# Latent attention: the products with the values taken for two query tiles at once, and the preparation of the next pair of heads moved to other steps

## The chip, the cores and the metric

One core of one Trainium2 chip. The time is device microseconds of one execution of the whole program, the median of three runs.

## What is computed

The program runs two layers of a hybrid attention network on 512 tokens, then two mixers that also carry a context of 256 tokens. The change is in the first of these, the latent mixer (MLA). Cut to what matters:

```
q = (rms_norm_2(cq, q_norm_g) @ w_uq).reshape(b, n, 16, 64 + 32)     # per head: 64 plain columns, 32 rotated
kv = (rms_norm_2(ckv, kv_norm_g) @ w_ukv).reshape(b, n, 16, 64 + 64) # keys (64, + 32 shared rotated) and values (64)
s = jnp.einsum('bqhrd,bkhd->bhrqk', qi, k) * scale                    # all keys, no mask
p = jax.nn.softmax(s, axis=-1)
o = jnp.einsum('bhrqk,bkhe->bqhre', p, v)
```

The 256 context queries attend to the 256 context keys; the 512 token queries attend to all 768 keys. All is float32.

## The kernel before, in words

The 16 heads are taken as eight head pairs `hp`. A head pair has five steps: step c (both context query tiles of 128 at once, 256 keys) and steps t0 to t3 (one tile of 128 token queries each, 768 keys). Four generators make the work of a step:

- `softmax` writes the scores of each of the two heads into a PSUM bank pair `S` (two buffers) with `mm3`, which multiplies two-part operands in three passes (lines 282 to 284). VectorE takes the row maximum (L1220), ScalarE the exponential (L1225), VectorE the reciprocal (L1227) and the scaling (L1230); the result is the tile `p`, queries down, keys across.
- `weigh` turns the `p` of the step before: TensorE transposes it in blocks of 128x128 into banks `T` (three buffers of one bank, L1245), ScalarE copies them to `pt` (L1246), and TensorE multiplies them with the values `V` into the bank `O` (one buffer, L1253): for each block of 128 keys one matmul per head, the two heads in the two halves of the array's columns, 64 value columns stationary, 128 queries moving. One such float32 matmul leaves two records in the trace. VectorE then multiplies `O` into the gate `sg` (L1260).
- `prepare(hp + 1)` makes the keys `kT` and queries `qT` of the next head pair: four matmul groups (six when the next pair is even, with a rotation of the queries on VectorE, L1176 to L1181), whose results go from a `T` bank through `split` (a copy on ScalarE, L253 or L256, then a difference on VectorE, L254 or L257) to SBUF. Four DMAs on SP's queue bring the rotated rows from `rot` into `qT`.
- `values` fills `V` before the first step.

The loop over steps calls these generators in turn: `next(sm)`, `next(ready)`, `next(w)`, twice a step. So the preparation of the next pair goes beside steps c, t0 and, if long, t1, until it is used up. A scheduler then sets each engine's order: an instruction that is ready may be moved ahead of one that waits. Engines run their own order strictly.

Names on the profile's rows: `S<-kT,qT` are scores; `T<-ident,p` transposes; `O<-pt,V` products with the values; `T<-ckT,spl` and `T<-cqT,spl` preparation. A similar scheme with two query tiles at a time stands already in the first layers' attention (`pt` with four blocks of 2x128, written at L521 and used at L528).

Of the kernel before, what the change touches and what calls it, by code (L numbers as in the profile page):

```python
# [10 lines left out]
F32 = mybir.dt.float32  # L11
# [3 lines left out]
AF = mybir.ActivationFunctionType  # L15
# [783 lines left out]
def alternate(*parts):  # L799
    parts = list(parts)  # L800
    while parts:
        parts = [p for p in parts if next(p, parts) is not parts]
# [256 lines left out]
def mla(P, xs, mod, H, before, keep):  # L1059

    nc, A = P.nc, P.A
# [13 lines left out]
    with ExitStack() as s1:  # L1075
# [33 lines left out]
        for j in range(8):  # L1109
            w = W().rearrange("p s (k n) -> p s k n", k=8)  # L1110
            for c, o, n in PARTS:
                ps = P.bankA()[:, 0:n]
                for k in range(8):
                    P.mm3(ps, w[:, 0, k], w[:, 1, k], *H.all(k, c), k == 0, k == 7)
                v = sg[j][:, o:o + n]
# [3 lines left out]
    before.close()  # L1119
    with st as s2:  # L1120
        P.psum(s2, S=(2, 2), T=(3, 1), O=(1, 1))
        kp, pp, one, qp = (P.pool(*x, s2) for x in (("m2k", 3), ("m2p", 3), ("m2o", 1), ("m2q", 4)))
        kTs = [one.tile([96, 2, 768], F32R, name=f"kT{i}") for i in (2, 3, 0, 1)]
        kTs = kTs[2:] + kTs[:2]
        tab = one.tile([128, 512], F32, name="tab")
# [1 line left out]
        V = [vp.tile([128, 1024], F32, name="V") for _ in range(6)]  # L1127
# [7 lines left out]
        for c, o, n in PARTS:  # L1135
            pt = P.bankT()
# [71 lines left out]
        def softmax(hp, c, t0):  # L1208
            two, m, c0 = (2, 256, 512) if c else (1, 768, 0)
            ps = []  # L1210
            for i in range(2):
                qT, kT = qTs[hp][i], kTs[(2 * hp + i) % 4]
                pss = P.bankS()
                for t in range(two):
                    q = slice(c0 + (t0 + t) * 128, c0 + (t0 + t + 1) * 128)
                    for o, w in ((512, 256),) if c else ((0, 512), (512, 256)):
                        d = pss[:, t * m + o - c0:t * m + o - c0 + w]
                        P.mm3(d, qT[:, 0, q], qT[:, 1, q], kT[:, 0, o:o + w], kT[:, 1, o:o + w], True, True)
                mx = P.sm.tile([128, 2], F32, name="mx")
                nc.vector.tensor_reduce(mx[:, 0:two], pss[:, 0:two * m].rearrange("p (t n) -> p t n", t=two),  # L1220
                                        AX.X, OP.max, negate=True)
                p = pp.tile([128, 768], F32, name="p")
                sl = P.sm.tile([128, 2], F32, name="sl")
                for t in range(two):
                    nc.scalar.activation(p[:, t * m:(t + 1) * m], pss[:, t * m:(t + 1) * m], AF.Exp,  # L1225
                                         bias=mx[:, t:t + 1], accum_out=sl[:, t:t + 1])
                nc.vector.reciprocal(sl[:, 0:two], sl[:, 0:two])  # L1227
                for t in range(two):
                    v = p[:, t * m:(t + 1) * m]
                    nc.vector.tensor_scalar(v, v, sl[:, t:t + 1], None, op0=OP.mult)  # L1230
                ps.append(p)
                yield ps

        def weigh(hp, c, t0, ps):
            two, m, c0 = (2, 256, 512) if c else (1, 768, 0)
            if t0 == 0:
                weigh.o = P.bankO()
            pts = []
            for p in ps:
                pt = kp.tile([128, 768], F32, name="pt")  # L1240
                for o in range(0, two * m, 512):
                    w = min(512, two * m - o)
                    pst = P.bankT()
                    for k in range(0, w, 128):
                        nc.tensor.transpose(pst[:, k:k + 128], p[:, o + k:o + k + 128], P.ident)  # L1245
                    nc.scalar.activation(pt[:, o:o + w], pst[:, 0:w], AF.Copy)  # L1246
                pts.append(pt)
                yield
            for t in range(two):
                for k in range(m // 128):  # L1250
                    for i in range(2):
                        h = 2 * hp + i
                        nc.tensor.matmul(weigh.o[64 * i:64 * i + 64, (t0 + t) * 128:(t0 + t + 1) * 128],  # L1253
                                         V[4 * c + k][:, h * 64:(h + 1) * 64],
                                         pts[i][:, t * m + k * 128:t * m + (k + 1) * 128],
                                         start=(k == 0), stop=(k == m // 128 - 1))
            n = 256 if c else 512
            if (t0 + two) * 128 == n:
                v = sg[hp][:, c0:c0 + n]
                nc.vector.tensor_tensor(v, v, weigh.o[:, 0:n], op=OP.mult)  # L1260
# [3 lines left out]
        for hp, c, t in steps:  # L1264
            if c:
                ready = prepare(hp + 1) if hp < 7 else iter(())
            sm = softmax(hp, c, t)
            w = weigh(*before) if before else iter(())
            next(w, None)
            for _ in range(2):  # L1270
                ps = next(sm)
                next(ready, None)
                next(w, None)
            before = (hp, c, t, ps)
        alternate(weigh(*before))


# [325 lines left out]
def program(tc, A, out):  # L1603
    with ExitStack() as ctx:
        P = Prog(tc, A, ctx)
        xs = [P.res.tile([128, 1024], F32, name=f"x{t}") for t in range(4)]
        before, keep = ExitStack(), ExitStack()
        H, mod = first_block(P, xs, P.pool("hx", 1, before))
        finish = mla(P, xs, mod.m[0], H, before, keep)
        gla(P, xs, finish, keep, mod.m[1], out)  # L1610
# [18 lines left out]
```

## Time and profile before

| what | value |
|---|---|
| median of 3 runs | 2325.97 us (2324.53 to 2327.81) |
| profiled execution, own time | 2323.18 us |
| its span, first to last instruction | 2321.4 us |
| TensorE busy | 2270.4 us, 98% |
| VectorE busy | 1477.5 us, 64% |
| ScalarE busy | 1064.0 us, 46% |
| latent mixer, first score to last product with values | 1674.96 to 1926.59 us |

Shares are means over the whole program, so the table says only which engine is busiest; the rows below are of the one stretch that the change touches.

### The profile page before, as it was taken

The numbers are of one execution on the slowest core, as the hardware profiler recorded it, in microseconds if no ns is written. First come the engines' busy times: TensorE is split into PE (matmuls) and PEld (weight loads), VectorE is DVE, ScalarE is ACT, GpSimd is POOL, SyncE is SP. The second block draws the span as 40 slices with busy tenths as digits, with TensorE's granted clock in tenths as the row PEclk, the third lists the DMA queues.
The fourth block names the chain that finished last, engine by engine and source line by source line (L and its number), as shares of the span: only waits on it lengthen the run. The fifth ranks groups of instructions, "written<-read, shape, count | busy, mean of one in ns | idle before, by whom it ended". The sixth has DMA issues, their size and how long they took to land.

```text
span 2321.4 us, 30494 instructions
## 1 busy us (share of the span) xinstructions
PE 2270.4 (98%) x11980; PEld 1866.9 (80%) x11980; DVE 1477.5 (64%) x2556; ACT 1064.0 (46%) x1958; POOL 71.4 (3%) x120
## 2 busy tenths in 40 slices
PE   8999999999999999999999999999999999999998
PEld 6777878888888777787888888888888888788886
DVE  4477795455555547779645556564477776756586
ACT  3366423444443336632344445452467773563332
POOL 0000000000000000000000000010000000000000
PEclk9999999999999999999999999999999999999999
DMA  4221464545542222146455554212110121121111
GB/s 154 82 75 54 156 214 139 173 127 156 170 100 91 83 82 82 46 163 214 131 178 126 159 165 116 92 54 71 50 31 20 26 74 37 53 83 37 55 47 72
DMA packets 61311, 234.37 MB, mean 101 GB/s; under 512 B 8544, under 2 KB 9840, under 8 KB 54768
## 3 DMA queue, kind: packets, MB, share of 16 engines
q1 hardware_dynamic: 50512, 179.99, 23.3%
q0 software_dynamic: 3456, 25.17, 6.0%
q10 hardware_dynamic: 7200, 27.27, 3.7%
q8 instruction: 94, 1.54, 0.3%
q14 instruction: 49, 0.40, 0.1%
HBM read 227.15 MB, written 2.10 MB: 99 GB/s over the span
## 4 chain that ended last, share of the span: by engine, by line
PE 69%; DVE 7%; ACT 2%; issue 2%; DMA 1%; POOL 1%; POOLq 0%; ACTq 0%; DVEq 0%; SPq 0%
PE A L282 14%; PE A L284 14%; PE A L283 14%; PE S L282 4%; PE S L283 4%; PE S L284 4%; PE O L1253 2%; PE T L1245 2%; DVE spl L254 1%; DMA ada<-in_ada 1%; PE O L284 1%; PE O L282 1%; PE O L283 1%; POOL rstd L293 1%; PE T L282 1%
## 5 line engine op out<-in xcount | busy, mean ns | idle before, releaser
L282 PE MATMUL A<-big,spl 128*128 128x512 f32 (+1 forms) x1280 | 482.3, 377 | 1.9 <-DVE x L777 1.2
L284 PE MATMUL A<-big,spl 128*128 128x512 f32 (+1 forms) x1280 | 479.9, 375 | 0.2 <-DVE spl L254 0.2
L283 PE MATMUL A<-big,spl 128*128 128x512 f32 (+1 forms) x1280 | 479.3, 375 | 0.0
L254 DVE TENSOR_TENSOR spl<-raw,spl 128x1024 fp32r<-128x1024 f32 (+2 forms) x265 | 317.2, 1200 | 181.4 <-ACT spl L253 179.6
L253 ACT ACTIVATE spl<-raw 128x1024 fp32r<-128x1024 f32 (+2 forms) x265 | 274.4, 1037 | 295.3 <-PE A L284 196.8
L282 PEld LDWEIGHTS A<-big,spl 128*128 128x128 f32 x1280 | 241.1, 188 | 47.3 <-issue 3.5
L284 PEld LDWEIGHTS A<-big,spl 128*128 128x128 f32 x1280 | 241.1, 188 | 43.8 <-issue 1.6
L283 PEld LDWEIGHTS A<-big,spl 128*128 128x128 f32 x1280 | 241.3, 188 | 41.1
L254 DVE TENSOR_TENSOR spl<-quarter,spl 128x1024 fp32r<-128x1024 f32 x84 | 102.2, 1223 | 144.5 <-ACT spl L253 144.5
L282 PE MATMUL A<-spl,big 128*128 128x512 f32 (+2 forms) x480 | 182.5, 383 | 7.4 <-ACT spl L253 3.4
L283 PE MATMUL A<-spl,big 128*128 128x512 f32 (+2 forms) x480 | 181.6, 379 | 0.5 <-DVE ms L291 0.5
L284 PE MATMUL A<-spl,big 128*128 128x512 f32 (+2 forms) x480 | 181.0, 378 | 0.2 <-DVE ms L291 0.2
L253 ACT ACTIVATE spl<-quarter 128x1024 fp32r<-128x1024 f32 x84 | 88.2, 1057 | 98.0 <-PE S L284 40.2
L282 PEld LDWEIGHTS A<-spl,big 128*128 128x128 f32 x480 | 90.1, 189 | 27.0 <-ACT spl L253 5.7
L283 PEld LDWEIGHTS A<-spl,big 128*128 128x128 f32 x480 | 90.6, 189 | 17.3 <-DVE spl L254 1.8
L284 PEld LDWEIGHTS A<-spl,big 128*128 128x128 f32 x480 | 90.5, 188 | 16.5 <-DVE ms L291 0.9
L282 PE MATMUL S<-spl,part 128*128 128x512 f32 x264 | 102.7, 389 | 0.0
L283 PE MATMUL S<-spl,part 128*128 128x512 f32 x264 | 102.7, 389 | 0.0
L284 PE MATMUL S<-spl,part 128*128 128x512 f32 x264 | 102.7, 389 | 0.0
L1220 DVE TENSOR_REDUCE mx<-S 128x1 f32<-128x768 f32 (+1 forms) x80 | 71.9, 900 | 26.3 <-PE S L284 25.5
L293 POOL TENSOR_TENSOR rstd<-ms,mhalf 128x1 f32<-128x1 f32 (+2 forms) x68 | 44.2, 650 | 1239.4 <-DVE ms L291 1194.0
L1246 ACT ACTIVATE pt<-T 128x512 f32<-128x512 f32 (+1 forms) x144 | 66.5, 501 | 32.0 <-PE T L1245 31.0
(442 smaller groups left out, 4329.1 us busy)
## 6 DMA issues: line engine op xcount, KB each, us to landing
raw<-in_wl SPq DMA_DIRECT2D x196, 512.0 KB, 4.0
ada<-in_ada ACTq DMA_DIRECT2D x48, 512.0 KB, 4.3
quarter<-in_wq SPq DMA_DIRECT2D x24, 1024.0 KB, 5.5
quarter<-in_wq POOLq DMA_DIRECT2D x24, 1024.0 KB, 9.0
raw<-in_gla SPq DMA_DIRECT2D x33, 512.0 KB, 3.8
raw<-in_mla SPq DMA_DIRECT2D x20, 512.0 KB, 3.6
raw<-in_mla SPq DMA_DIRECT2D x8, 384.0 KB, 3.0
qT<-rot SPq DMA_DIRECT2D x32, 96.0 KB, 2.8
```

The lines of the kernel that those rows point to most:

```text
L253: nc.scalar.activation(hi, src, AF.Copy)
L254: nc.vector.tensor_tensor(lo, src, f32(hi), op=OP.subtract)
L282: mm(ps, lh, rh, start=start, stop=False, **more)
L283: mm(ps, lh, rl, start=False, stop=False, **more)
L284: mm(ps, ll, rh, start=False, stop=stop, **more)
L293: nc.gpsimd.tensor_tensor(r, ms, self.mhalf[:, 0:w], op=OP.pow)
L1220: nc.vector.tensor_reduce(mx[:, 0:two], pss[:, 0:two * m].rearrange("p (t n) -> p t n", t=two), AX.X, OP.max, negate=True)
L1245: nc.tensor.transpose(pst[:, k:k + 128], p[:, o + k:o + k + 128], P.ident)
L1246: nc.scalar.activation(pt[:, o:o + w], pst[:, 0:w], AF.Copy)
L1253: nc.tensor.matmul(weigh.o[64 * i:64 * i + 64, (t0 + t) * 128:(t0 + t + 1) * 128], V[4 * c + k][:, h * 64:(h + 1) * 64], pts[i][:, t * m + ...
```

## The change

`weigh` keeps one pair of `pt` tiles for two token steps (shape 128 x 6 x 2 x 128: key block, tile, query) and multiplies only in steps with odd `t0`, for both query tiles at once: 256 queries moving per matmul. Step c does the same with its two tiles. The pool of `pt` tiles grows from three of 768 to four of 1536 columns. In the loop, `ready` (the preparation) is no longer advanced in step c, in step t2, and in step t0 of even pairs; what is left of it after step t3 is drained there. `weigh` runs one step late, so the products of t0 and t1 fall in step t2, and those of t2 and t3 in the next pair's step c.

```diff
-        kp, pp, one, qp = (P.pool(*x, s2) for x in (("m2k", 3), ("m2p", 3), ("m2o", 1), ("m2q", 4)))
+        kp, pp, one, qp = (P.pool(*x, s2) for x in (("m2k", 4), ("m2p", 3), ("m2o", 1), ("m2q", 4)))
...
-            pts = []
-            for p in ps:
-                pt = kp.tile([128, 768], F32, name="pt")
+
+            if t0 % 2 == 0:
+                weigh.pts = [kp.tile([128, 6, 2, 128], F32, name="pt") for _ in range(2)]
+            pts = weigh.pts
+            for p, pt in zip(ps, pts):
...
-                    nc.scalar.activation(pt[:, o:o + w], pst[:, 0:w], AF.Copy)
-                pts.append(pt)
+                    if c:
+                        d, v = pt[:, 0:2], pst.rearrange("p (t k n) -> p k t n", t=2, k=2)
+                    else:
+                        d, v = pt[:, o // 128:(o + w) // 128, t0 % 2], pst[:, 0:w].rearrange("p (k n) -> p k n", n=128)
+                    nc.scalar.activation(d, v, AF.Copy)
                 yield
-            for t in range(two):
+            if c or t0 % 2:
+                q = slice(0, 256) if c else slice((t0 - 1) * 128, (t0 + 1) * 128)
                 for k in range(m // 128):
                     for i in range(2):
                         h = 2 * hp + i
-                        nc.tensor.matmul(weigh.o[64 * i:64 * i + 64, (t0 + t) * 128:(t0 + t + 1) * 128],
-                                         V[4 * c + k][:, h * 64:(h + 1) * 64],
-                                         pts[i][:, t * m + k * 128:t * m + (k + 1) * 128],
+                        nc.tensor.matmul(weigh.o[64 * i:64 * i + 64, q], V[4 * c + k][:, h * 64:(h + 1) * 64],
+                                         pts[i][:, k].rearrange("p t n -> p (t n)"),
...
+            busy = c or t == 2 or (t == 0 and hp % 2 == 0)
             for _ in range(2):
                 ps = next(sm)
-                next(ready, None)
+                if not busy:
+                    next(ready, None)
                 next(w, None)
+            if t == 3:
+                for _ in ready:
+                    pass
```

Counted in TensorE's order over the stretch (a block is a run of products with the values that nothing interrupts):

| | before | after |
|---|---|---|
| products with the values | 448 of 128 queries | 224 of 256 queries |
| blocks | 56 | 34 |
| blocks with an odd number of products | 32 | 20 |
| blocks entered from scores or preparation / from transposes | 53 / 3 | 29 / 5 |
| blocks left into scores or preparation / into transposes | 32 / 24 | 16 / 18 |

**Inside a head pair.** TensorE, first head pair, the change of step from t2 to t3; before:

```order
L1245 MATMUL T<-ident,p 128x128 x6
L282 MATMUL S<-kT_12798,qT 128x512
L283 MATMUL S<-kT_12798,qT 128x512
L284 MATMUL S<-kT_12798,qT 128x512
L282 MATMUL S<-kT_12798,qT 128x256
L283 MATMUL S<-kT_12798,qT 128x256
L284 MATMUL S<-kT_12798,qT 128x256
L1253 MATMUL O<-pt,V 64x128 x12
L282 MATMUL S<-kT_12795,qT 128x256
```

and now, in the same head pair, where the products of t0 and t1 stand in step t2:

```order
L1247 MATMUL T<-ident,p 128x128 x6
L282 MATMUL S<-kT_12798,qT 128x256
L283 MATMUL S<-kT_12798,qT 128x256
L284 MATMUL S<-kT_12798,qT 128x256
L1259 MATMUL O<-pt,V 64x256 x12
L1247 MATMUL T<-ident,p 128x128 x6
L282 MATMUL S<-kT_12797,qT 128x512
L283 MATMUL S<-kT_12797,qT 128x512
L284 MATMUL S<-kT_12797,qT 128x512
```

The same twelve products are twice as wide and stand once where they stood twice; three scores now lie between the last transposes and the first product instead of six.

**The first step of all.** TensorE, the scores of step c of the first head pair and what follows; before:

```order
L283 MATMUL T<-ckT,spl 128x512
L284 MATMUL T<-ckT,spl 128x512
L282 MATMUL S<-kT_12798,qT 128x256
L283 MATMUL S<-kT_12798,qT 128x256
L284 MATMUL S<-kT_12798,qT 128x256
L282 MATMUL S<-kT_12798,qT 128x256
L283 MATMUL S<-kT_12798,qT 128x256
L284 MATMUL S<-kT_12798,qT 128x256
L1245 MATMUL T<-ident,p 128x128 x4
```

and now:

```order
L284 MATMUL S<-kT_12797,qT 128x256
L282 MATMUL S<-kT_12798,qT 128x256
L283 MATMUL S<-kT_12798,qT 128x256
L284 MATMUL S<-kT_12798,qT 128x256
L282 MATMUL S<-kT_12798,qT 128x256
L283 MATMUL S<-kT_12798,qT 128x256
L284 MATMUL S<-kT_12798,qT 128x256
L1247 MATMUL T<-ident,p 128x128 x4
```

The seven matmuls of preparation between the scores of the first head and those of the second (the last two are shown) are gone from there.

**From an odd head pair to the next.** TensorE, the end of step t3 of the second head pair and step c of the third; before:

```order
L284 MATMUL S<-kT_12796,qT 128x256
L1245 MATMUL T<-ident,p 128x128 x6
L1253 MATMUL O<-pt,V 64x128
L282 MATMUL S<-kT_12797,qT 128x256
L283 MATMUL S<-kT_12797,qT 128x256
L1253 MATMUL O<-pt,V 64x128 x11
L1245 MATMUL T<-ident,p 128x128 x6
```

and now:

```order
L284 MATMUL T<-cqT,spl 128x512
L1247 MATMUL T<-ident,p 128x128 x12
L1259 MATMUL O<-pt,V 64x256
L282 MATMUL S<-kT_12797,qT 128x256
L283 MATMUL S<-kT_12797,qT 128x256
L284 MATMUL S<-kT_12797,qT 128x256
L282 MATMUL S<-kT_12797,qT 128x256
L283 MATMUL S<-kT_12797,qT 128x256
L284 MATMUL S<-kT_12797,qT 128x256
L1259 MATMUL O<-pt,V 64x256 x11
```

Preparation now ends right ahead of the transposes, and the transposes of both heads follow each other; this stands so at the end of the second, fourth and sixth head pair.

## Rows read from the trace of the kernel before

**Rows 1.** The page: the span, and TensorE's busy time, share and instructions

```profile
span 2321.4 us, 30494 instructions
PE 2270.4 (98%) x11980; PEld 1866.9 (80%) x11980; DVE 1477.5 (64%) x2556; ACT 1064.0 (46%) x1958; POOL 71.4 (3%) x120
```

**Rows 2.** Busy time of PE, PEld, DVE, ACT, POOL in the stretch; then TensorE's clock

```profile
1674.96:1926.59 251.63, 249.03 (x2088) 209.63 (x2086) 193.05 (x367) 183.53 (x417) 0.00 (x0) 1.00 0.14 35
```

**Rows 3.** Timeline of TensorE around one block: start us, us, engine line op

```profile
1818.33 0.28 PE L283 MATMUL S<-kT,qT 96*128 96x256 f32 x1
1818.45 0.28 PE L284 MATMUL S<-kT,qT 96*128 96x256 f32 x1
1818.66 1.53 PE L1253 MATMUL O<-pt,V 128*64 128x128 f32 x24
1820.12 0.50 PE L282 MATMUL S<-kT,qT 96*128 96x512 f32 x1
1820.46 0.40 PE L283 MATMUL S<-kT,qT 96*128 96x512 f32 x1
1820.69 0.82 PE L1245 MATMUL T<-ident,p 128*128 128x128 f32 x6
1821.27 0.48 PE L284 MATMUL S<-kT,qT 96*128 96x512 f32 x1
```

**Rows 4.** Timeline of TensorE at shorter blocks, each with what follows it

```profile
1804.18 0.43 PE L1253 MATMUL O<-pt,V 128*64 128x128 f32 x2
1804.54 0.50 PE L282 MATMUL S<-kT,qT 96*128 96x512 f32 x1
...
1813.91 1.09 PE L1253 MATMUL O<-pt,V 128*64 128x128 f32 x16
1814.93 0.87 PE L1245 MATMUL T<-ident,p 128*128 128x128 f32 x6
1815.56 0.48 PE L282 MATMUL S<-kT,qT 96*128 96x512 f32 x1
```

**Rows 5.** The two-tile scheme of the first layers, timeline of TensorE

```profile
148.71 0.65 PE L528 MATMUL O<-pt,av 128*64 128x256 f32 x2
149.28 0.71 PE L618 MATMUL S<-mv,kC 128*128 128x129 f32 x4
```

**Rows 6.** Groups on ScalarE by shape: xcount | busy us, mean ns | idle before

```profile
L521 ACT ACTIVATE pt<-T 128x512 f32<-128x512 f32 x16 | 9.5, 595 | 6.0 <-PE T L520 6.0
L1246 ACT ACTIVATE pt<-T 128x512 f32<-128x512 f32 x80 | 47.8, 598 | 32.0 <-PE T L1245 31.0
L1246 ACT ACTIVATE pt<-T 128x256 f32<-128x256 f32 x64 | 24.3, 380 | 0.0
L1225 ACT ACTIVATE p<-S,mx 128x768 f32<-128x768 f32 x64 | 57.8, 903 | 13.6 <-DVE mx L1220 12.8 <-DVE sl L1227 0.3
L1225 ACT ACTIVATION_READ_ACCUMULATOR p<-S,mx 128x1 f32 x96 | 19.3, 201 | 0.0
L253 ACT ACTIVATE kT<-T 64x512 fp32r<-64x512 f32 x14 | 8.3, 594 | 7.9 <-DVE kT L254 4.5 <-PE T L284 3.4
L253 ACT ACTIVATE kT<-T 64x256 fp32r<-64x256 f32 x14 | 5.3, 379 | 2.6 <-PE T L284 2.4
```

**Rows 7.** Timeline at the first step: scores, then transposes waiting for `p`

```profile
1675.56 0.28 PE L284 MATMUL S<-kT,qT 96*128 96x256 f32 x1
...
1675.68 0.28 PE L284 MATMUL T<-ckT,spl 128*128 128x256 f32 x1
...
1678.41 0.63 PE L1245 MATMUL T<-ident,p 128*128 128x128 f32 x4 [0.35 <-DVE p L1230]
```

**Rows 8.** Timeline at the last head pair's last step

```profile
1918.69 0.82 PE L1245 MATMUL T<-ident,p 128*128 128x128 f32 x6
...
1920.48 1.53 PE L1253 MATMUL O<-pt,V 128*64 128x128 f32 x24
...
1922.41 0.85 PE L1245 MATMUL T<-ident,p 128*128 128x128 f32 x6 [0.41 <-DVE p L1230]
```

**Rows 9.** Who waited for whom in the stretch: total us, times, longest us

```profile
PEld O L1253 <- ACT pt L1246: 1.3, 4, 0.4
```

**Rows 10.** DMA issues of the page: KB each, us to landing

```profile
qT<-rot SPq DMA_DIRECT2D x32, 96.0 KB, 2.8
```

## The prediction

> **What bounds the kernel now.** I read the page first: TensorE is busy 98% of the span [rows 1], so a gain has to come out of TensorE's own time or out of its few waits. Then I cut out the stretch that the change touches, from the first score of the latent mixer to its last product with the values: 251.6 us, in which TensorE is busy 249.0, VectorE 193.1 and ScalarE 183.5, at a granted clock of 1.00, the upper of its two levels (2.4 GHz) [rows 2]. TensorE waits only 2.6 us there; a better spread of the preparation can give back no more than that. But "busy" counts an instruction until its results are out, so it hides what TensorE loses between instructions of different kinds. For that I read start times in the timeline.
>
> Scores of 256 columns start 0.12 us apart; ahead of a block of products with the values it is 0.21. A block of 24 records (12 products) takes 1.46 us from its first start to the next instruction's start. The first score behind it then takes 0.34 instead of 0.23 [rows 3]. A block of 8 products takes 1.02 and one single product 0.36 [rows 4]. Four products more cost 0.44 us, so a product costs 0.11, and a block has 1.46 - 12 x 0.11 = 0.15 that belongs to no product. In a single one the partner in the other half of the array is missing: 0.36 = 2 x 0.11 + 0.15, so a block with an odd number pays for one more. Altogether each block costs TensorE 0.15 inside, 0.09 at its entry from scores and 0.11 at its exit into scores; into transposes it is 0.05 (six transposes take 0.63 behind a block and 0.58 behind a score [rows 3, 4]). I look for what the change does to the number of blocks and to the waits.
>
> **The products.** A product of 256 moving queries is not in this stretch, but the first layers have it: one alone takes 0.57 us to the next start [rows 5], 0.21 more than one of 128, so 0.105 more per slot and 0.215 for a slot of 256. Before: 448 products and 32 odd blocks make 480 slots x 0.11, and 56 blocks x 0.15: 52.3 (with 0.109 unrounded) + 8.4 = 60.7 us. After: (224 + 20) x 0.215 + 34 x 0.15 = 52.5 + 5.1 = 57.6. That is -3.1.
>
> The row says that width is paid in full: half as many products with half as many weight loads, and nothing saved by that. The Trainium skill (TensorE: Matmul & The Clock Gate, section "Back-to-back issue gap") says otherwise of a stream of weight loads and matmuls: about 81 ns for 128 columns and 131 for 512, so twice the width costs far less than twice the time. An estimate from that page, some 98 ns for 256 columns, would shrink the wide slot to 0.13 and the sum by another 20 us; the row disagrees, and it decides here.
>
> **The edges.** By the counts of the order, entries from scores or preparation fall from 53 to 29: 24 x 0.09 = -2.2. Exits into them fall from 32 to 16: 16 x 0.11 = -1.8. Exits into transposes fall from 24 to 18: 6 x 0.05 = -0.3. Entries from transposes rise from 3 to 5, +0.2 at the same 0.09. Sum -4.1; with the products **-7.2 us**. The remaining matmuls (scores, transposes, preparation) are the same in number and width.
>
> **The copies to `pt`.** They now write four runs of 128 apart. L521 does just that and takes 595 ns, L1246 in one run 598 [rows 6]: nothing. The larger pool frees tiles two steps later at most; with four buffers the next pair of tiles is free before it is asked for, so I price it at nothing. If it were not, the transposes would wait for a wide block, 2.7 us, up to 24 times, and TensorE's order has at least one step of other work between these.
>
> **The preparation that moves.** Its matmuls, its `split` copies and its rotation cost what they did; what counts is what lies beside them. In a token step ScalarE has two exponentials with their accumulator reads, 2 x (0.903 + 0.201), two pairs of copies, 2 x (0.598 + 0.380), and, where `kT` or `qT` is prepared, 2 x (0.594 + 0.379): 2.2 + 2.0 + 1.9 = 6.1 us [rows 6]. TensorE has in step t1 of such a step, now without products, two heads of scores at 3 x (0.23 + 0.12) each, 12 transposes at 0.11 and a preparation of 6 x (0.23 + 0.12): 2.1 + 1.3 + 2.1 = 5.5. So ScalarE is 0.6 us behind there, once in a head pair, and has it back in t2, where TensorE has 2.7 us of wide products. The scores have two buffers, so I take that lag as hidden; uncovered it is 0.6 x 7 = 4 us. The DMAs of the rotated rows, four a head pair and 2.8 us each to landing [rows 10], start about a step later on SP's queue. Behind them stand the loads of the next weights. Two steps of over 5 us cover both; without that cover it would be 2.8 us at each of seven pairs.
>
> **Where cover is gone.** Three places.
> - First step: the first transposes need `p`, and `p` comes 1678.41 - 1675.68 = 2.7 us after the first head's scores, of which 0.35 is shown as idle [rows 7]. Seven matmuls of preparation, some 1.5 us, lay in between. They are now done later, at no less cost, so the wait grows by 1.5.
> - Last step: from the end of the scores at 1918.69 to the transposes at 1922.41 it is 3.7 us, covered by 0.6 of transposes, 1.2 of scores and a block of 1.46, with 0.41 idle [rows 8]. That block has now been done one step before. The wait grows by up to 1.46; I take 1.2, as some of the 3.7 is ScalarE's and VectorE's own queue, which is shorter then.
> - Behind t3 of the second, fourth and sixth pair, twelve transposes follow each other. They need four `T` banks, of which three exist, one of them just filled by preparation. The second six wait for the first copy, 0.6 us [rows 6], and the wide block then for its own behind a `split` of 0.6. Bounds 0 and 1.2 each; I take 0.5, since the block in that place is already cut in two now: +1.5.
>
> Against this, of the 2.6 us of idle that exist I give back 1, those beside the steps where preparation and products stood together. Waits: 1.5 + 1.2 + 1.5 - 1.0 = **+3.2 us**.
>
> **Sum.** -7.2 + 3.2 = -4.0 us. The profiled execution took 2323.2 by its own clock; it becomes 2319.2. It stands 2.8 us below the median of the runs, so in these the forecast is **2322 us**. A change under 0.2% (4.65 us) can hardly be told from none on this kernel.
>
> **Rivals.**
> - A, the waits don't grow: the scheduler moves whatever is ready into the gaps, as it does now with 2.6 us of idle in 251.6 [rows 2]. Then the whole -7.2 shows, with up to 1 or 2 us of the idle on top: -6 to -9, about 2319 (2317 to 2320). For it: the small idle of today. Against it: the places above have little left that is ready.
> - B, slower: the wide block waits for ScalarE. Its second product needs the second head's copy, and now only three scores (0.4 us) lie behind the transposes at the place shown in step t2, instead of six (1.1). If an exponential, 1.1 us with its read, stands ahead of that copy in ScalarE's order, each of 16 wide blocks waits 1.1: +17.6 - 7.2 = +10.4, 2336. The gain is gone from 0.45 us a block on, and it shows as slower from 0.74. Against it: such a wait came 4 times in the stretch, 1.3 us in all [rows 9]; ScalarE is busy 73% of it. For it: in t1 and t3 ScalarE has as much to do as TensorE. The Trainium skill (TensorEngine Tiling (Array Packing), "Performance Considerations") warns of just this for matmuls in column tiles: they get faster and the emptying of PSUM does not.
> - C, nothing is left: the lag in t1 isn't hidden (4 us) and the three places cost their upper bounds (1.5 + 1.5 + 3.6). That gives -7.2 + 4 + 6.6 = +3.4 at most, else around -1: 2322 to 2329, no change that shows.
> - D, weight loads set the pace: if a slot stayed at 0.11 with 256 columns, 244 x 0.105 = 26 us more would go, 2293. Only [rows 5] speak to it, and against it.
>
> **Chances.** Forecast (-1 to -5.5) 0.47, A 0.30, C 0.13, B 0.08, D 0.02. Faster by over 0.2%: A, D and the part of the forecast beyond -4.65 (0.08): 0.40. Slower: B, 0.08. The rest, 0.52, within 0.2%. The range takes the forecast, A and C: from 2317 to 2329. It leaves out B and D.
>
> **What the profile after would show.** The stretch should be about 247.5 us long. A block of 24 records of 256 columns should take 12 x 0.215 + 0.15 = 2.7 us; if it takes under 2, D is right. Some 34 blocks should stand in the timeline, with 0.2 to 0.3 us lost at each. The first transposes of the stretch should wait about 2 us, the last head pair's 1.6, and those behind t3 of even pairs little. If the products wait for `pt` more than 7 us in all, B has happened. If ScalarE's copies come on time and TensorE's idle in the stretch stays at 2 to 3 us, A has. I am wrong in the main if the rest of the program, whose order is the same, moves by more than 1 us.

## The result: slower, and where the profile after shows it

The changed kernel takes 2340.51 us (2338.68 to 2343.74, four runs), the kernel before, beside it on the same chip, 2326.89 (2324.53 to 2328.04). The ratio is 1.0063, its 95% interval 1.0051 to 1.0075: slower by 13.6 us, where 4 us faster was forecast and a chance of 0.08 was given to slower. The two profiled executions lie further apart, 2340.8 and 2323.2, as the one of the kernel before was 2.8 us under its median.

The page and then the windows view of the changed kernel, over the same stretch as [rows 1, 2], from the first score to the last product; columns as there:

```profile
span 2339.0 us, 29589 instructions
PE 2275.8 (97%) x11532; PEld 1854.5 (79%) x11532; DVE 1477.5 (63%) x2556; ACT 1062.2 (45%) x1958; POOL 71.4 (3%) x120
...
1675.03:1942.95 267.92, 252.47 (x1644) 196.18 (x1643) 194.10 (x369) 182.25 (x417) 0.00 (x0) 0.99 0.13 33
```

The stretch begins at the same time (1675.0) and is 16.3 us longer, 267.9 in place of 251.6. VectorE and ScalarE are as busy as before. TensorE's idle, length less busy time, goes from 2.6 to 15.5 us.

The timeline of TensorE in the first pairs of the changed kernel (answers to [rows 3, 4]; start us, us, engine line op, and in brackets the idle before it with its releaser):

```profile
1727.71 2.81 PE L1259 MATMUL O<-pt,V 128*64 128x256 f32 x24
1730.45 0.50 PE L282 MATMUL S<-kT,qT 96*128 96x512 f32 x1
...
1735.36 0.36 PE L284 MATMUL S<-kT,qT 96*128 96x256 f32 x1
1736.13 0.50 PE L282 MATMUL T<-cqT,spl 128*128 128x512 f32 x1 [0.41 <-ACT pt L1252]
...
1738.32 0.82 PE L1247 MATMUL T<-ident,p 128*128 128x128 f32 x6
1739.65 0.87 PE L1247 MATMUL T<-ident,p 128*128 128x128 f32 x6 [0.51 <-ACT pt L1252]
1740.45 0.65 PE L1259 MATMUL O<-pt,V 128*64 128x256 f32 x2
1741.03 0.39 PE L282 MATMUL S<-kT,qT 96*128 96x256 f32 x1
...
1742.10 2.80 PE L1259 MATMUL O<-pt,V 128*64 128x256 f32 x22
1746.24 0.63 PE L1247 MATMUL T<-ident,p 128*128 128x128 f32 x4 [1.34 <-DVE p L1230]
```

A block of twelve products takes 1730.45 - 1727.71 = 2.74 us and a single one 0.58, as forecast (2.73 and 0.58). From 1735 on stands the end of step t3 of the second pair. TensorE waits there three times: the preparation comes 0.77 behind the score ahead of it in place of 0.12, the second six transposes 1.33 behind the first in place of 0.66, and the transposes of step c 4.14 behind a block of 2.74. That is 2.7 us; the places behind the fourth and sixth pair cost about as much, some 8.5 us in all.

Why `p` is late there stands in VectorE's timeline, with the end of ScalarE's exponentials below it:

```profile
1742.81 0.69 DVE L1220 TENSOR_REDUCE mx<-S 128x2 f32<-128x512 f32 x1
1744.94 0.69 DVE L1265 TENSOR_TENSOR sg<-sg,O 128x512 f32<-128x512 f32 x1 [1.43 <-PE O L1259]
1745.54 0.16 DVE L1227 RECIPROCAL sl<-sl 128x2 f32<-128x2 f32 x1
1745.73 0.62 DVE L1230 TENSOR_SCALAR p<-p,sl 128x256 f32<-128x256 f32 x2
...
1744.36 0.20 ACT L1225 ACTIVATION_READ_ACCUMULATOR p<-S,mx 128x1 f32 x1
```

The exponentials are done at 1744.56. But in VectorE's order the product with the gate `sg` stands ahead of the reciprocal, and it waits for the wide block to end: some 1.0 of the 1.34 us. Behind the sixth pair it stands between the reciprocal and the scaling, and the transposes wait 1.14. Behind the fourth it stands after the scaling, and they wait 0.07; there the products wait 0.75 for `pt` and the scores 0.79 for a bank.

The same view at the first step and the last pair (answers to [rows 7, 8]):

```profile
1676.57 0.28 PE L284 MATMUL S<-kT,qT 96*128 96x256 f32 x1
1678.33 0.70 PE L1247 MATMUL T<-ident,p 128*128 128x128 f32 x4 [1.48 <-DVE p L1230]
...
1681.56 0.63 PE L283 MATMUL S<-kT,qT 96*128 96x512 f32 x1
1681.98 0.63 PE L284 MATMUL S<-kT,qT 96*128 96x512 f32 x1
1682.41 0.41 PE L282 MATMUL S<-kT,qT 96*128 96x256 f32 x1
...
1935.72 1.09 PE L1247 MATMUL T<-ident,p 128*128 128x128 f32 x6 [1.87 <-DVE p L1230]
```

The waits have grown from 0.35 to 1.48 and from 0.41 to 1.87. Behind the first, scores of 512 columns start 0.42 apart, where they start 0.23 apart elsewhere. The windows view tells why; the number behind POOL is the granted clock:

```profile
1681.00:1684.00 3.00, 3.00 (x13) 2.67 (x13) 1.49 (x5) 1.04 (x3) 0.00 (x0) 0.57 0.00 0
1937.00:1940.00 3.00, 3.00 (x11) 1.78 (x9) 0.02 (x1) 1.16 (x4) 0.00 (x0) 0.57 0.03 5
```

For some 3 us behind each of these waits TensorE has mostly the lower of its two levels, 1.2 GHz.

The view of who waited for whom over the stretch, first of the changed kernel (us in total, times, longest):

```profile
ACT p L1225 <- DVE mx L1220: 26.3, 33, 2.4
...
PE T L1247 <- DVE p L1230: 6.8, 8, 1.9
PEld S L282 <- ACT p L1225: 5.9, 7, 1.4
...
PEld O L1259 <- ACT pt L1252: 5.7, 12, 1.0
...
PE S L282 <- ACT p L1225: 2.9, 5, 1.2
...
PE T L282 <- ACT pt L1252: 2.1, 7, 0.4
...
PE T L1247 <- ACT pt L1252: 1.5, 3, 0.5
...
PE O L1259 <- ACT pt L1252: 1.3, 2, 0.7
```

and of the kernel before, where [rows 9] has the last kind with 1.3:

```profile
ACT p L1225 <- DVE mx L1220: 12.8, 24, 1.2
...
PEld S L282 <- ACT p L1225: 2.0, 3, 1.0
...
PE S L282 <- ACT p L1225: 1.3, 3, 0.8
...
PE T L1245 <- DVE p L1230: 1.0, 3, 0.4
```

The rows of PEld are the weight loads, which run beside the matmuls; the idle of the matmuls themselves is in the rows of PE. Most of its growth is not the products waiting for `pt` (1.3 us). It is transposes waiting for `p`, and scores waiting for a score bank that the exponential hasn't read yet: two ends of the softmax chain, 9.7 us in place of 2.3. Another 4.9 us, where the kernel before has next to none, end with ScalarE's copies to `pt`: preparation and transposes waiting for a bank, and products.

### The profile page after: what moved, and what is told of

Same layout as the page of the kernel before. It is cut to its first block, busy times and chain, and to the rows that moved or that the text cites. A ratio compares the mean times of both kernels' runs of the same rounds, so it can differ in the third digit from the quotient of the medians.

```text
span 2339.0 us, 29589 instructions
## 1 busy us (share of the span) xinstructions
PE 2275.8 (97%) x11532; PEld 1854.5 (79%) x11532; DVE 1477.5 (63%) x2556; ACT 1062.2 (45%) x1958; POOL 71.4 (3%) x120
## 4 chain that ended last, share of the span: by engine, by line
PE 83%; DVE 9%; ACT 4%; DMA 2%; issue 2%; POOL 1%; SPq 0%; ACTq 0%; POOLq 0%; DVEq 0%
PE A L282 18%; PE A L283 18%; PE A L284 18%; PE S L282 4%; PE S L284 4%; PE S L283 4%; PE O L1259 2%; PE T L1247 2%; DVE spl L254 1%; PE O L528 1%; PE S L498 1%; DMA raw<-in_wl 1%; PE T L520 1%; ACT spl L253 1%; POOL rstd L293 1%
## 5 line engine op out<-in xcount | busy, mean ns | idle before, releaser
L1225 ACT ACTIVATE p<-S,mx 128x768 f32<-128x768 f32 (+1 forms) x96 | 72.5, 759 | 27.5 <-DVE mx L1220 26.3
```

## The experiments

Two theories at first: M, that the moved preparation uncovers this chain, and W, that the wide products do. All results in one table; stretch and idle are read as above, from one profiled execution each, and a ratio is to the kernel before in the same job.

| run | median us | ratio (95%) | stretch us | idle us |
|---|---|---|---|---|
| before | 2324 to 2327 | | 251.6 | 2.6 |
| the change | 2340.5 | 1.0063 (1.0051 to 1.0075) | 267.9 | 15.5 |
| e1_wide | 2340.7 | 1.0065 (1.0053 to 1.0078) | 266.8 | 14.2 |
| e2_move | 2333.9 | 1.0039 (1.0027 to 1.0052) | 263.2 | 8.4 |
| e3_ends | 2336.2 | 1.0046 (1.0032 to 1.0060) | 263.7 | 13.1 |
| e4_c | 2336.6 | 1.0046 (1.0034 to 1.0059) | 264.7 | 12.1 |
| e5_spread | 2329.6 | 1.0023 (1.0014 to 1.0031) | 256.9 | 2.2 |
| e6_free_after | 2340.7 | 1.0066 (1.0053 to 1.0078) | 267.8 | 15.4 |
| e7_free_before | 2325.7 | 1.0001 (0.9992 to 1.0010) | 251.6 | 2.5 |
| e8_filler | 2338.0 | 1.0059 (1.0045 to 1.0073) | 265.0 | 14.0 |
| e9_short_wide | 2320.7 | 0.9977 (0.9968 to 0.9987) | 248.2 | 4.7 |
| e10_short_after | 2329.5 | 1.0015 (1.0005 to 1.0024) | 254.6 | 9.0 |
| e11_short_before | 2318.2 | 0.9963 (0.9951 to 0.9976) | 243.4 | 1.2 |
| e12_bunch | 2325.3 | 0.9999 (0.9990 to 1.0008) | 251.3 | 2.4 |
| e13_t2 | 2346.0 | 1.0090 (1.0077 to 1.0104) | 269.4 | 15.2 |
| e14_both | 2341.4 | 1.0068 (1.0055 to 1.0082) | 267.8 | 12.8 |
| e15_last | 2337.4 | 1.0057 (1.0045 to 1.0070) | 264.6 | 12.8 |

**One half of the change each.** Diffs are against the changed kernel. e1_wide keeps the wide products and puts the preparation back:

```diff
-            busy = c or t == 2 or (t == 0 and hp % 2 == 0)
...
-                if not busy:
-                    next(ready, None)
+                next(ready, None)
...
-            if t == 3:
-                for _ in ready:
-                    pass
```

> The wide products alone, with the preparation where it was before (beside steps c, t0 and, if long, t1). Theory M (the moved preparation is what uncovers the chain from scores to p): TensorE keeps its cover in step c, the wide products give their -7.2 us, the stretch is 244 to 248 us long, the time 2318 to 2323. Theory W (the width is what uncovers it: steps t1 and t3 have no products any more): the stretch stays at 260 to 270 us, the time at 2334 to 2342. If both are needed together (theory I), 250 to 256 us and 2325 to 2331.

e2_move is the kernel before with these lines added and nothing else of the change.

> The move alone: products of 128 queries in every step as before, the preparation by the new rule (none in step c, t2 and t0 of even pairs, the rest drained after t3). Theory M: the stretch grows by 12 to 20 us over the 251.6 of before, to 264 to 272, time 2337 to 2346, with the idle behind step c. Theory W: every step still has its block of products as cover, so 251 to 254 us and 2325 to 2329, but for about 2 us at the first step. Theory I: 253 to 258 us.

Each half alone is slower, by 15.2 and 11.5 us in the stretch, and both together by hardly more, 16.3. W's numbers for the width came true; M's for the move all but (263.2 for 264 at least, and 2333.9 for 2337). In the profiled execution of e2_move an estimated 3 of its 11.5 us are the clock, which stands at 0.52 and 0.50 in two windows of 3 us behind the first wait; by the medians e2_move is 8.8 slower. So neither theory alone holds: each edit takes something out of steps that need it. In e1_wide the wait has one form that comes back pair after pair, in the steps without products. TensorE's, VectorE's and ScalarE's timeline there:

```profile
1757.52 0.48 PE L282 MATMUL S<-kT,qT 96*128 96x512 f32 x1
...
1758.53 0.28 PE L284 MATMUL S<-kT,qT 96*128 96x256 f32 x1
1759.45 0.50 PE L282 MATMUL S<-kT,qT 96*128 96x512 f32 x1 [0.64 <-ACT p L1225]
...
1757.14 0.96 DVE L1220 TENSOR_REDUCE mx<-S 128x1 f32<-128x768 f32 x1 [0.37 <-PE S L284]
...
1757.64 0.87 ACT L1252 ACTIVATE pt<-T 128x512 f32<-128x512 f32 x2 [0.22 <-PE T L1247]
1758.40 0.90 ACT L1225 ACTIVATE p<-S,mx 128x768 f32<-128x768 f32 x1
```

The score bank asked for at 1758.65 is the one that VectorE's maximum begins to read at 1757.14 and that the exponential still reads until 1759.3. The maximum is done at 1758.1; the 0.3 us to the exponential are ScalarE's copies to `pt`, so a part of this chain is its queue. Six transposes and six scores of the other head are all that TensorE has in between. In the kernel before, a block of 1.46 us stands there.

**Places.** e3_ends restores the first pair's preparation and the last pair's narrow products; e4_c gives step c its preparation back:

```diff
-            busy = c or t == 2 or (t == 0 and hp % 2 == 0)
+            busy = hp and (c or t == 2 or (t == 0 and hp % 2 == 0))
...
-            if c or t0 % 2:
+            if c or t0 % 2 or hp == 7:
```

```diff
-            busy = c or t == 2 or (t == 0 and hp % 2 == 0)
+            busy = t == 2 or (t == 0 and not c)
```

> The change, but with the old places of the preparation in the first head pair and products of 128 queries in the token steps of the last head pair. All theories: the idle of 1.6 us at the first transposes and of 2.0 and 1.3 in the last pair is gone. If the half clock behind these waits is their consequence, the granted clock stays at its upper level (2.4 GHz) at both ends and another 3 us come back: the stretch goes from 267.9 to 259 to 262 us, with about 1 us paid for the narrow products. If the clock falls for another reason, it still falls there, and the stretch is 263 to 266 us. If the waits only go elsewhere, 267 to 268.

> The change, but the preparation goes beside steps c, t1 and, if long, t3, so that step c has it again. Theory M: the waits of 0.7 and 1.4 us behind t3 of the second, fourth and sixth pair and that of the first step go, 10 us in all with the clock at the first step: the stretch is 256 to 261 us, the time 2328 to 2333. Theory W: no change but at the first step, 264 to 268 us. If step t3 of even pairs, which has neither products nor preparation here, opens instead, each of four opens by 1 to 2 us, and 260 to 266 come out.

e3_ends: 263.7. The clock stays at 1.00 at both ends, but 4.3 us come back where 6 to 9 were expected. e4_c: 264.7. The long waits at the first step and ahead of step c's transposes are gone. Step t3 of the odd-numbered pairs (first, third, ...), now bare, opens instead: the scores behind it wait 0.6 to 0.7 us for a bank. That is the third case of its expectation with smaller waits; the stretch alone fits theory W as well (264 to 268).

**Width without bunching.** e5_spread cuts each wide block in two halves that stand in successive steps:

```diff
+            if weigh.rest:
+                weigh.rest()
+                weigh.rest = None
+            if c:
+                weigh.rest = lambda: part(range(2))
+            elif t0 % 2:
+                part(range(3))
+                weigh.rest = lambda: part(range(3, 6))
```

> Wide products as in the change, but each block of twelve is cut in two halves of six, one in each of two steps, and those of step c go to step t1, so that every token step and step c has some; the preparation where it was before. If the loss comes from cover that is bunched in every second step, the stretch is back at 249 to 253 us and the time at 2322 to 2327; 16 more blocks than in the change cost some 5 us of the 7.2. If products of 256 queries or the copies that write four runs cause waits of their own wherever they stand, it stays at 260 us or more, 2334 and up.

The idle is 2.2 us, less than before: with some products in every step the waits are gone, though the products are as wide as in the change. What is left is the products' own price. It has 60 blocks, 38 of them odd: (224 + 38) x 0.215 + 60 x 0.15 = 65.3 us, 4.6 over the 60.7 of before; the stretch is 5.3 longer, over the range given, because I had reckoned with 50 blocks.

**The exponential freed from the maximum.**

```diff
-                                         bias=mx[:, t:t + 1], accum_out=sl[:, t:t + 1])
+                                         bias=P.zero, scale=2.0 ** -10, accum_out=sl[:, t:t + 1])
```

> The change, but the exponential no longer reads the row maximum: it takes the scores times 1/1024, and the maxima are still computed and read by nobody (so the output is another softmax). All engines have the same work; only the chain from scores to p and to a free score bank is shorter, by the 0.96 us of the maximum. If the length of that chain is what the uncovered steps wait for, the stretch falls from 267.9 to 246 to 254 us. If ScalarE's or VectorE's amount of work per step is the bound, it stays at 262 us or more.

> The kernel before with the same edit, as the control: it has 2.6 us of idle in the stretch, so both theories expect 249 to 252 us. What counts is the difference between the two freed kernels: -7 to +2 us if the chain is the cause (the saving of 7.2 shows once the chain is covered), +10 to +16 if the work is.

Nothing moved, and the waits view of e6_free_after says why these two decide nothing:

```profile
ACT p L1225 <- DVE mx L1220: 26.8, 33, 2.4
```

The exponential no longer reads the maximum and waits for it as before, as both read the same score bank. The Trainium skill (PSUM — Partial Sum Buffer, section "PSUM bank collisions raise a hardware error ⚠️") says that the compiler orders any two engines at one bank, readers too; this row agrees. So the edit had to take VectorE off the bank. Once it is off, in e10_short_after below, the row of the exponential waiting for `mx` is gone.

**The chain shortened.** In e9_short_wide (on e1_wide), e10_short_after and e11_short_before (control):

```diff
-                nc.vector.tensor_reduce(mx[:, 0:two], pss[:, 0:two * m].rearrange("p (t n) -> p t n", t=two),
+                nc.vector.tensor_reduce(mx[:, 0:two], V[0][:, 0:two * m].rearrange("p (t n) -> p t n", t=two),
...
-                                         bias=mx[:, t:t + 1], accum_out=sl[:, t:t + 1])
+                                         bias=P.zero, scale=2.0 ** -10, accum_out=sl[:, t:t + 1])
```

> Wide products alone (as e1_wide), and the maximum out of the chain: VectorE's reductions read 768 columns of V in place of the scores, and the exponential takes the scores times 1/1024 without a maximum (another softmax). VectorE and ScalarE have the same instructions; from scores to a free score bank only the exponential is left, some 1 us less. If the length of the chain is what the steps without products wait for, TensorE's idle falls from 13 to 2 to 5 us and the stretch from 266.8 to 249 to 255 us. If the amount of work on ScalarE or VectorE is the bound, it stays at 262 us or more.

> The change with the same edit. If the chain is the cause: 246 to 254 us in the stretch in place of 267.9, and the waits of the transposes for p and of the scores for a free bank shrink to a third. If the work is the bound: 262 us or more.

> The kernel before with the same edit, the control: 248 to 252 us by both theories. With the chain as the cause, the change is then -6 to +3 us against this control in the stretch; with the work as the cause, +10 or more.

A reduction still takes 937 ns (954 before). The wide products alone lose 18.6 us of stretch and come within 4.8 of the control, where they were 15.2 above: there the chain is the cause, for about two thirds. One thing differs from the expectation. Nothing holds these reductions in their places any more, and they run early (their row, and then the windows of the third and fourth pair in e9_short_wide and in e1_wide):

```profile
L1220 DVE TENSOR_REDUCE mx<-V x80: 661/934/954, 1657.8 to 1803.7; 128x1 f32<-128x768 f32 x64, 128x2 f32<-128x512 f32 x16
...
1734.61:1799.14 64.53, 63.23 (x425) 49.03 (x424) 61.49 (x114) 45.27 (x107) 0.00 (x0) 1.00 0.11 22
...
1738.94:1806.47 67.53, 64.55 (x423) 49.83 (x423) 49.79 (x96) 44.82 (x105) 0.00 (x0) 1.00 0.12 27
```

In these pairs VectorE has more to do than in e1_wide (61.5 us busy for 49.8), and TensorE is idle less (1.3 for 3.0). So it is not the amount of VectorE's work that holds e1_wide up.

The whole change was 16.3 above and is 11.2 above the control, over the bound of 10 set for the other theory: in the bare difference the chain explains some 5 us of it. The order of the blocks changed too. By the product sum e10_short_after, with 38 blocks and 26 odd ones, pays 59.5 us, 2.0 more than its control, where the change pays 3.1 less than before. Without the products' price 9.2 us are lost in place of 19.4, so an estimate of the chain's part is one half. The waits view of e10_short_after shows what is left:

```profile
PEld O L1259 <- ACT pt L1252: 8.9, 16, 1.7
PE O L1259 <- ACT pt L1252: 3.9, 5, 1.2
...
PE T L1247 <- DVE p L1230: 2.0, 3, 1.1
```

The waits for `p` are down from 6.8 to 2.0, and the products wait for ScalarE's copies instead, 5.7 to 8.9: 0.5 to 1.2 us of idle at a time in the same three places behind t3, where the `split` copies of the preparation in t3 and of the next weights, the transposes' copies and the exponentials all fall to ScalarE. (The control itself gains 8.3 us: 1.4 of idle, and 49 blocks with 12 odd, 57.5 us in place of 60.7; the rest I did not trace.)

**Late, but narrow.** e12_bunch is e1_wide with the twelve products of each tile kept apart, still both in every second step:

```diff
+                for t in range(2):
+                    o = (0 if c else t0 - 1) + t
...
-                        nc.tensor.matmul(weigh.o[64 * i:64 * i + 64, q], V[4 * c + k][:, h * 64:(h + 1) * 64],
+                            nc.tensor.matmul(weigh.o[64 * i:64 * i + 64, o * 128:(o + 1) * 128],
```

> Wide products undone, but the products of two tiles still stand together in every second step as narrow ones, and the preparation is where it was before. Narrow products of the first tile are ready a step earlier, and the scheduler's order does draw 5 to 7 of the 24 forward. If it is only the late place of the products that costs, the stretch stays at 262 to 267 us as in e1_wide. If the joining of two tiles in one product is what keeps them from filling a gap, it is 251 to 257 us.

As the kernel before, idle included. The first tile's products are ready a step early and are put into the gaps; a wide product isn't ready before the second tile. It takes few of them: counted between the scores, step t1 of the first six pairs has 3 to 7 products and step t2 17 to 21. The run also writes the same runs of 128 into the same larger pool of `pt`, so neither of these costs anything that shows.

**The wait and the clock.** e8_filler adds work to the first step:

```diff
+                if c and hp == 0:
+                    extra = P.bankT()
+                    for k in range(2):
+                        P.mm3(extra, ckT[:, 0, k, 0:128], ckT[:, 1, k, 0:128],
+                              ckT[:, 0, k, 0:512], ckT[:, 1, k, 0:512], k == 0, k == 1)
```

> The change with twelve needless matmuls of 512 columns more in the first step of the first head pair, 2.8 us of TensorE's time, whose results nobody reads; nine of them stand between the scores and the first transposes, where TensorE waited 1.6 us. If the half clock that follows there comes from the wait, it goes: the granted clock stays at 2.4 GHz, and the stretch is 1 to 3 us shorter than the 267.9 in spite of 2.1 us of added work. If the clock falls anyway, the stretch is 268 to 270 us. The last pair's wait and clock stay as they are.

265.0, 2.9 us shorter with 2.1 us more work in it. Its windows at the two ends, and TensorE's timeline at the last:

```profile
1681.00:1684.00 3.00, 3.00 (x19) 1.95 (x17) 2.26 (x5) 2.46 (x5) 0.00 (x0) 1.00 0.00 0
1936.00:1939.00 3.00, 3.00 (x23) 1.72 (x24) 1.35 (x2) 1.53 (x3) 0.00 (x0) 1.00 0.02 5
...
1934.00 0.41 PE L1247 MATMUL T<-ident,p 128*128 128x128 f32 x2 [1.87 <-DVE p L1230]
```

At the first step the wait is gone and the clock stays up; from the first score to the preparation's first wait, 14.3 us in the change and 12.9 here, 1.4 come back net of the added 2.1. The other 1.6 come at the last step, where nothing was changed: the same 1.87 us of wait stands there, but in this execution the clock did not fall behind it.

**The three places behind t3, and the last pair.** e13_t2 takes the last two groups of the even-numbered pairs' preparation from t3 to t2, e15_last only makes the last pair narrow (the second half of e3_ends), e14_both is e3_ends and e13_t2:

```diff
-            busy = c or t == 2 or (t == 0 and hp % 2 == 0)
+            busy = c or t == (3 if hp % 2 else 2) or (t == 0 and hp % 2 == 0)
```

> The change, but in pairs whose next pair needs six matmul groups the last two go to step t2 (beside the wide products) in place of t3, so nothing is drained behind t3 and the transposes there no longer follow it. The trace of the change loses about 2.9 us at each of three such places (0.65 where the preparation waits for a bank, 0.67 between the transposes, 1.4 before those of step c). If the place of the preparation ahead of the copies is the cause, 4 to 8 us come back: 260 to 264 us in the stretch. If every step that has neither products nor preparation pays, t3 now pays instead: 265 to 269 us.

> The change with narrow products in the token steps of the last head pair alone. There the change waits 1.3 and 2.0 us and then runs 3 us at a lower granted clock. If that is what the last pair's wide products cost, 2.5 to 4.5 us come back, after 1 to 1.5 us more for the narrow ones: 263.5 to 265.5 us in the stretch. If the waits stay, 268 to 269 us.

> The same with the old places of the preparation in the first head pair and narrow products in the last one (as e3_ends). If the three causes add up, the stretch is that of e3_ends (263.7 us) less what e13_t2 gives: 255 to 260 us. It cannot come under the 251.7 of before unless the shorter product time of 57.6 us in place of 60.7 is not eaten by waits; I expect it slower than before.

e13_t2 is the slowest of all (269.4, 0.4 over what was expected of a bare t3). In the fourth pair TensorE's timeline has this, and the window behind it:

```profile
1803.84 0.28 PE L284 MATMUL S<-kT,qT 96*128 96x256 f32 x1
1806.39 0.88 PE L1247 MATMUL T<-ident,p 128*128 128x128 f32 x6 [2.27 <-DVE p L1230]
...
1807.00:1810.00 3.00, 3.00 (x18) 2.63 (x18) 1.18 (x2) 1.77 (x5) 0.00 (x0) 0.59 0.15 53
```

Without preparation t3 is bare, the transposes wait 2.2 to 2.8 us for `p` in the three places, and the clock falls behind each. So the preparation there was cover more than trouble. e15_last gives 3.3 us back, as expected. e14_both doesn't add up, 267.8 in place of 255 to 260: the three waits behind t3 stand as in e13_t2, with the lower clock behind each. No version here that keeps the row maximum in the softmax beats the kernel before; e12_bunch equals it.

## Why the prediction was wrong, step by step

**What bounds the kernel** was read rightly: TensorE's own time and its few waits. **The products** came out as summed: blocks of 2.74, 0.58 and 1.01 us, 34 of them, 57.6 us; e5_spread confirms the sum from the other side. Width is paid in full. **The copies** that write four runs take 594 ns (598 before), as said. **The edges** are smaller than said: by an estimate from the undisturbed start intervals of all other matmuls in the stretch (each kind at its lower quartile) they give some -2 us for -4.1. So about 5 us were saved and 16.3 + 5 = some 21 lost.

**"Where cover is gone"**, the +3.2 us, is the step that failed: the sum of waits was mis-sized, some 21 us lost in its place, and it rests on a premise that does not hold.

- First step: +1.5 said, the wait grew by 1.1, from the cause named. Not priced was the lower clock behind it, some 1.5 us (1680.03 to 1683.67 by start times, against the same instructions elsewhere).
- Last step: +1.2 said, "up to 1.46"; it grew by 1.46. Not named were another wait of 1.3 us one step earlier and again the clock, 1.6 (against e8_filler, where it did not fall). By e15_last, where the clock stays up, the last pair's wide products cost 3.3 net.
- Behind t3 of the second, fourth and sixth pair: +1.5 said, at most 3.6; some 8.5 measured. I had the second six transposes waiting for a bank (0.5 said, 0.67) but not that the preparation itself waits there first (0.65), nor that the next pair's step c, which has lost its preparation just as the first step has, then finds `p` late by 1.4, with the gate's product in VectorE's way.
- The other token steps: taken as none, with 1.0 given back. Some 5 us are left here, 2.7 of them idle in short waits (0.55 at most) for ScalarE's copies and for `p`. How the 5 us come about is not shown.
- The premise was that a step with 2.7 us of products once and none the other time is covered on the mean. With two score banks it isn't where the lean step has nothing else: VectorE and ScalarE can't run ahead in the full step, and the bare one runs at the pace of the chain (e1_wide against e5_spread and e9_short_wide). In the change itself the moved preparation fills these steps but in the last pair, which has none.

**ScalarE's lag in t1** (0.6, called hidden) stayed nearly hidden: in the steps t1 the change has 1.0 us of idle in all eight pairs. **Rivals**: B's time (2336) came nearest, not its mechanism. Products waited for `pt` 5.7 us, not the 17.6 it needs, and under the 7 named as its mark, and in TensorE's own idle it is 1.3; it appears where e10_short_after has shortened the chain. A and C asked for waits of 0 to 11 us and are out, D is out by the block of 2.74. **The rest of the program** takes 1.2 us longer behind the stretch, more than the 1 named as a sign; over all these kernels this part varies from 393.1 to 397.4 us, so it is none.

Not settled: how the losses behind t3 divide between the softmax chain, VectorE's order and ScalarE's queue. Shortening the chain showed the queue, and no run put the gate's product behind the scaling.

## What to carry to other kernels

Where a chain through several engines returns to TensorE within a step, list per step what TensorE has to do that doesn't depend on it, and compare it with the chain (here 2.7 to 3.7 us) step by step, not on the mean: here two score banks carried no surplus over. Look, too, for instructions that stand in the chain's engines ahead of it and wait for TensorE themselves, as the gate's product did. Joining two small products into one saves edges, about 5 us here, but the joined one is ready only with its last input; products that are ready early are what closes gaps. And a wait may cost more than its length, by what runs behind it at the lower clock.

## What the runs showed of the hardware that was not expected

Behind a single wait of TensorE of 1.5 to 2.8 us the granted clock fell to the lower level for some 3 us in several places (0.57 in the change, 0.59 in e13_t2), which cost about 1.5 us at each end of the change; in e2_move it stayed down for about twice as long. Behind the same wait of 1.87 us it fell in the change and in e4_c, and not in e1_wide, e6_free_after, e8_filler and e13_t2. Nine needless matmuls put into such a wait made the stretch 2.9 us shorter, though only 1.4 of that belong to them.

An exponential whose operand VectorE no longer makes still waited for VectorE (26.8 us in all, 26.3 before the edit), as long as both read one score bank.
